# A two-layer hybrid trunk on one core: modulation sums by ones, rows ahead of weights, and rows on GpSimd's queue

## The chip, the core and the metric

The kernel runs on one core of a Trainium2 chip. A core has a matrix engine (TensorE, PE in the profile, whose weight loads are listed as PEld), a vector engine (VectorE, DVE), an activation engine (ScalarE, ACT), GpSimd (POOL) and a queue engine (SyncE, SP) that here does nothing but issue DMAs. Each engine takes its own instructions strictly in the order of its own list. Sixteen DMA engines move the data for all queues. The metric is the device time in microseconds, lower is better. It stands at 2661.34 us, the median of three runs (2660.47 to 2666.17).

## The reference, cut to what matters

```python
cond = jax.nn.silu(c)                                   # (1, 2048)
for l in range(2):
    mod = cond @ w_ada[l] + b_ada[l]                    # 6 vectors of 2048
    sh_m, sc_m, gt_m, sh_f, sc_f, gt_f = mod            # shift, scale, gate
    u = x * (1 + sc_m) + sh_m                           # x: (256, 2048)
    proj = u @ w_in[l]                                  # 4896 columns
    mix = concat(window_attention(proj), rwkv7(proj)) @ w_out[l]
    x = layer_norm(alpha * x + gt_m * mix)
    u = x * (1 + sc_f) + sh_f
    gate, up = split(u @ w_gate_up[l])                  # 2 x 5632 columns
    x = layer_norm(alpha * x + gt_f * ((silu(gate) * up) @ w_down[l]))
```

All weights are float32 and each is used once. `w_ada` alone is 2 x 2048 x 12288 numbers, 201 MB of the 622 MB that are read.

## The kernel before, in words

**Products.** Each float32 weight tile is split into a rounded part `hi` (ACT, line 430) and a remainder `lo` (DVE, line 431), and the activations are held as two such parts too. A product is three matmuls: high by high, high by `lo`, and the activation's remainder by high. `steps` (from line 415) loads a `raw` tile of 128 x 1024 (four buffers), makes `hi` (three buffers) and `lo` (two buffers), yields them to the matmuls, and then calls `pump`. `stream` (line 439) uses the weights as the moving operand, 512 columns at a time: lines 452, 453 (the one that reads `lo`) and 455. A step of two 512-column pieces and two token tiles is 12 matmuls. `tstream` (lines 464 to 466) uses the weights as the stationary operand.

**Modulation rows.** The six vectors per layer are not computed by matmul but on DVE: a tile `ast` holds 128 rows of `w_ada`, and `aacc += ast * cond[j]` runs once per row tile (line 265, in the opening line 353). 16 row tiles make one half of one vector, a unit. The sum over the 128 partitions follows in `ada_sums` (line 311): PE transposes each 128-column block (line 322), ACT sums each transposed block along its free side (line 326, one activation and one read of its accumulator), and DVE adds the bias (line 329) into `mods`. `pump` draws row tiles from one long generator at a set pace, so that the rows lie beside the weight streams: 0.75 of a draw per step in the feed-forward. The generator draws 20 times for a unit, of which 16 issue a row tile. `aacc` has one buffer in the feed-forward. An `ast` tile has two; its DMA stands on SP's queue (line 261), between the weights' DMAs (line 422).

**The opening.** The first two vectors of layer 0 (shift and scale) are needed before any matmul of `w_in`. `parts` (line 1355) makes them in five parts of 512, 512, 512, 256 and 256 columns. `ada_first` (line 340) loads the rows of both vectors of a part (line 348, eight buffers), DVE adds them up, `ada_sums` closes each vector, `make_u` transposes x and makes the activations `u` (lines 404 to 411), and `front` (line 513) runs the matmuls of that part over the 1696 columns that it holds.

**Order.** The program is built by a scheduler that orders instructions on every engine by its own simulated timeline, unless a dependence holds one back. So SP's queue is one list, in which rows, weights and small loads are mixed.

**Later.** In the mixer of layer 0 two units run by matmul instead (`ada_direct`, line 285: `cond` spread over 32 columns as stationary operand, the row tile as moving one, four at a time in four column groups of the array). `channel` holds the output projection and the feed-forward. Layer norm's reciprocal root is a power on GpSimd (line 1130), which does nothing else in the feed-forward.

Of the kernel before, what the change touches and what calls it, by code (L numbers as in the profile page):

```python
# [10 lines left out]
F32 = mybir.dt.float32  # L11
# [8 lines left out]
P = 128  # L20
D = 2048
# [23 lines left out]
PARTS = (4, 4, 4, 2, 2)  # L45
LAG = 2
WB = (4, 3, 2)
RED = 1
AR = (3, 7)
AA = (1, 45)  # L50
AP = (0.65, 0.3)
# [11 lines left out]
SPLIT_D = (1, 1)  # L63
WOFF, WPAD = 16, 64
TWO_PI = 2.0 * math.pi
IDLE = {"ada": 0, "first": 0, "dec": (0, 0), "ffn": (11, 6), "mix": 8}


@with_exitstack
def hybrid_trunk_kernel(  # L70
# [98 lines left out]
    def drv(l, nm, i, n=1):  # L169
        return der[l][:, DO[nm] + i:DO[nm] + i + n]  # L170

    def setup(sp, l, half, behind=None):

        prow = sp.tile([P, P], F32, tag="prow", bufs=2, name=f"prow{l}{half}")
# [76 lines left out]
    def ada_steps(l, mod, c0):  # L251

        src = w_ada[l].rearrange("(j p) n -> p j n", p=P)
        n0 = mod * D + c0
        if direct[0]:
            yield from ada_direct(l, mod, c0, src[:, :, n0:n0 + 1024])
            return
        acc = adap.tile([P, 1024], F32, tag="aacc", name="aacc")
        for j in range(KT):
            t = adap.tile([P, 1024], F32, tag="ast", name="ast", bufs=2)  # L260
            dma(t, src[:, j, n0:n0 + 1024])
            if j == 0:
                V.tensor_scalar_mul(acc, t, cond[:, 0:1])
            else:
                ins = V.scalar_tensor_tensor(acc, t, cond[:, j:j + 1], acc, ALU.mult, ALU.add)  # L265
# [6 lines left out]
        ada_sums(l, mod, c0, [acc[:, i * P:(i + 1) * P] for i in range(8)])  # L272
        done.add((l, mod, c0 // 1024))
        yield

    def ada_direct(l, mod, c0, src):
# [21 lines left out]
        row = adap.tile([P, T], F32, tag="aacc", name="grow")  # L298
        S.copy(row, gv[:, 0:T])
        turn[:] = 1, 1  # L300
        b = bank()
        for i in range(2):
            PE.transpose(b[:, i * P:(i + 1) * P], row[:, i * P:(i + 1) * P], ident)
        col = mod * KT + c0 // P
        bv = b[:, 0:T].rearrange("p (i q r) -> p q i r", q=4, r=32)
        V.scalar_tensor_tensor(mods[l][:, col:col + 8].rearrange("p (q i) -> p q i", q=4), bv[:, :, :, 0], 1.0 if mod in (1, 4) else 0.0,
                               prm(l, "b_ada", col, 8).rearrange("p (q i) -> p q i", q=4), ALU.add, ALU.add)
        done.add((l, mod, c0 // 1024))
        yield

    def ada_sums(l, mod, c0, blocks, idle=0):

        col = mod * KT + c0 // P
        n = len(blocks)
        sm = adap.tile([P, 8], F32, tag="asum", name="asum", bufs=2)
        for q in range(0, n, 4):
            b = bank()
            if q == 0:
                warm(b, idle)
            m = min(4, n - q)  # L320
            for i in range(m):
                PE.transpose(b[:, i * P:(i + 1) * P], blocks[q + i], ident)  # L322
            for i in range(m):
                bi = b[:, i * P:(i + 1) * P]
                if RED:
                    S.activation(bi, bi, AF.Copy, accum_out=sm[:, q + i:q + i + 1])
            if not RED:
                V.reduce_sum(sm[:, q:q + m], b[:, 0:m * P].rearrange("p (i k) -> p i k", k=P), axis=AX.X)
        V.scalar_tensor_tensor(mods[l][:, col:col + n], sm[:, 0:n], 1.0 if mod in (1, 4) else 0.0,
                               prm(l, "b_ada", col, n), ALU.add, ALU.add)  # L330
        if mod in (2, 5):
            row = adap.tile([8, P], F32, tag="arow", name="arow", bufs=2)[0:n]
            rb = bank()
            PE.transpose(rb[0:n, 0:P], mods[l][:, col:col + n], ident)
            S.copy(row, rb[0:n, 0:P])
            dma(gates[l, mod // 3, c0 // P:c0 // P + n], row)

    lead = []

    def ada_first(pool, c0, w):  # L340

# [3 lines left out]
        for j0 in range(0, KT, jj):  # L345
# [6 lines left out]
                else:  # L352
                    V.scalar_tensor_tensor(acc, t[:, j], cond[:, j0 + j:j0 + j + 1], acc, ALU.mult, ALU.add)
            yield
        for m in range(2):
            ada_sums(0, m, c0, [acc[:, m, i * P:(i + 1) * P] for i in range(w // P)], IDLE["ada"] if m == 0 and c0 + w == D else 0)

    done = set()

# [13 lines left out]
                       + halves(1, 5))  # L373
    pace = [0.0, 0.0]
    anchor = []
    direct = [False]

    def pump():

# [34 lines left out]
    def steps(srcs, W, kts, room=None, off=0):  # L414
# [3 lines left out]
        for i0 in range(0, len(kts), no):  # L418
            m = min(no, len(kts) - i0)
            raw = wp.tile([P, 1024], F32, tag="raw", name="raw", bufs=WB[0])  # L420
            for dst, src in srcs(raw[:, 0:m * W].rearrange("p (k w) -> p k w", w=W), kts[i0], m):
                dma(dst, src)
            if room:
                parts = [(raw[:, o * W:(o + 1) * W], *room()) for o in range(m)]
            else:
# [11 lines left out]
                    yield i0 + o, hi[:, o * W:(o + 1) * W], lo[:, o * W:(o + 1) * W]  # L437
            pump()

    def stream(srcs, W, kts, lhs, pieces, banks, first=True, last=True, ts=(0, 1), room=None, held=None):  # L440


        kept = []
        for i, hi, lo in held or steps(srcs, W, kts, room):
            kept.append((i, hi, lo))
            lt = lhs[i]
            st, sp_ = first and i == 0, last and i == len(kts) - 1
            for t in ts:
                xh, xl = lt[:, 0, t * P:(t + 1) * P], lt[:, 1, t * P:(t + 1) * P]
                for q, (c0, w) in enumerate(pieces):  # L450
                    bt = banks[t][q][:, 0:w]
                    PE.matmul(bt, lhsT=xh, rhs=hi[:, c0:c0 + w], start=st, stop=False)  # L452
                    PE.matmul(bt, lhsT=xh, rhs=lo[:, c0:c0 + w], start=False, stop=False)  # L453
                for q, (c0, w) in enumerate(pieces):
                    PE.matmul(banks[t][q][:, 0:w], lhsT=xl, rhs=hi[:, c0:c0 + w], start=False, stop=sp_)  # L455
        return kept

    def tstream(srcs, W, kts, us, blocks, first=True, last=True):
# [81 lines left out]
    def mixer(l, us, mixp, feeds):  # L540
# [99 lines left out]
        def decays(g):  # L640

            gsl = slice(g * T, (g + 1) * T)
            w2a2 = pa.tile([P, T], F32, tag="w2a2", name="w2a2", bufs=1)
            dma(w2a2[0:64, :], rwkv_w2[l, :, gsl])
            dma(w2a2[64:128, :], rwkv_a2[l, :, gsl])
# [534 lines left out]
    def channel(l, ys, wa, fp):  # L1180
# [77 lines left out]
                dma(out[0, t * P:(t + 1) * P, o:o + 512], zq)  # L1258

        gtf = fp.tile([P, D], F32, tag="gt", name="gtf")  # L1260
        wg = w_gate_up[l].rearrange("(k p) (s n) -> p k s n", p=P, s=2)
        first = True
        for lo_g, hi_g in ((0, 6), (6, 11)):
# [42 lines left out]
            for c0, w in ((0, 1024), (1024, 512), (1536, 512)):  # L1306
# [11 lines left out]
                for ts in ((0,), (1,)) if apart else ((0, 1),):  # L1318
# [5 lines left out]
                    for t in ts:  # L1324
# [8 lines left out]
                        if c0 == 1536 and not first:  # L1333
                            finish(t) if l + 1 == L else normalise(fp, z, t, stt[t])
            first = False
        if l + 1 == L:
            return None, None
        us = []
# [12 lines left out]
    with tc.tile_pool(name="pro", bufs=1) as pp:  # L1351
        xv = x[0].rearrange("(t p) d -> p t d", p=P)

        def parts():
# [23 lines left out]
            zt = pp.tile([P, 520], F32, name="zt")  # L1378
            G.memset(zt, 0.0)
            for t in tinv:  # L1380
                dma(t.rearrange("e s t -> (e s t)").rearrange("(p n) -> p n", p=P), zt)
# [38 lines left out]
```

## Time and profile before

| | us |
|---|---|
| median of three runs | 2661.34 |
| the profiled execution, its own time | 2673.23 |
| span of the profiled execution, first to last instruction | 2671.2 |
| PE busy | 2514.0 (94%) |
| VectorE busy | 1804.7 (68%) |
| ScalarE busy | 1186.5 (44%) |
| GpSimd busy | 146.7 (5%) |

The profiled execution is 11.9 us longer than the median and 2.0 us longer than its span. Read it by stages: the opening, up to the decays of the first mixer, where rows arrive; mixer 0, to 560; its output projection, to 640; the feed-forward of layer 0, 640 to 1400; mixer 1 and its projection; the feed-forward of layer 1, from 1960. Modulation rows run in the first four and in mixer 1 up to some 1700; in the last feed-forward there are none.

### The profile page before, as it was taken

What the parts mean: (1) busy time and instruction counts of PE and PEld (TensorE: products, weight loads), DVE (VectorE), ACT (ScalarE), POOL (GpSimd) and SP (SyncE); (2) the same over time, 40 slices, a digit from 0 to 9 for tenths busy, and PEclk for the clock granted to TensorE, in tenths of its full rate; (3) what the DMA queues carried; (4) which work ended last, traced back from release to release, by engine and by line L of the source; (5) the groups of instructions that cost most, each with busy time, mean ns of one, the idle gap of its engine ahead of it and who ended that gap; (6) DMA issues with size and microseconds to landing.
All of it is one profiled execution on the core that took longest, in us unless ns stands there. A gap on an engine that the chain in (4) does not pass through costs nothing.

```text
span 2671.2 us, 42267 instructions
## 1 busy us (share of the span) xinstructions
PE 2514.0 (94%) x15619; PEld 2090.1 (78%) x15619; DVE 1804.7 (68%) x2439; ACT 1186.5 (44%) x2023; POOL 146.7 (5%) x368
## 2 busy tenths in 40 slices
PE   3799998999999999999999998989899999999997
PEld 3697785677878888888788977867788888888887
DVE  7977766579877777677787776564855455545456
ACT  2464454435544444444454644543444443344442
POOL 1002212000000000000000024110000000000000
PEclk9899998999999999999999999988999999999999
DMA  9978658698998889888878785414655655566654
GB/s 371 358 215 253 202 176 266 207 335 301 327 328 303 309 301 317 284 299 304 293 247 291 218 264 148 129 50 179 221 189 184 195 184 196 195 190 188 191 189 149
DMA packets 336384, 637.51 MB, mean 239 GB/s; under 512 B 59510, under 2 KB 126514, under 8 KB 334642
## 3 DMA queue, kind: packets, MB, share of 16 engines
q1 hardware_dynamic: 333170, 629.05, 71.0%
q0 software_dynamic: 1280, 2.62, 0.4%
q10 hardware_dynamic: 1728, 3.15, 0.3%
q8 instruction: 122, 2.00, 0.3%
q14 instruction: 84, 0.69, 0.1%
HBM read 622.08 MB, written 12.62 MB: 238 GB/s over the span
## 4 chain that ended last, share of the span: by engine, by line
PE 62%; DMA 6%; DVE 5%; ACT 1%; issue 1%; POOL 0%; SPq 0%; DVEq 0%; ACTq 0%; POOLq 0%
PE acc L453 18%; PE acc L455 17%; PE acc L452 17%; DMA ast<-in_w_ada_dram 3%; DVE lo L431 2%; PE acc L465 1%; PE acc L466 1%; PE acc L464 1%; DMA raw<-in_w_gate_up_dram 1%; DVE aacc L265 1%; PE mb L1290 1%; DMA raw<-in_w_out_dram 1%; DMA raw<-in_w_in_dram 1%; PE mb L322 0%; DMA tm<-tinv 0%
## 5 line engine op out<-in xcount | busy, mean ns | idle before, releaser
L430 ACT CAST hi<-raw 128x1024 fp32r<-128x1024 f32 (+2 forms) x728 | 758.2, 1044 | 1093.2 <-PE acc L455 826.5
L431 DVE TENSOR_TENSOR lo<-raw,hi 128x1024 fp32r<-128x1024 f32 (+2 forms) x728 | 880.4, 1212 | 519.0 <-PE acc L453 350.1
L453 PE MATMUL acc<-lo,u 128*128 128x512 f32 x1568 | 515.7, 396 | 14.3 <-DVE lo L431 14.3
L455 PE MATMUL acc<-hi,u 128*128 128x512 f32 x1568 | 508.1, 392 | 0.0
L452 PE MATMUL acc<-hi,u 128*128 128x512 f32 x1568 | 460.1, 395 | 0.7 <-ACT u L410 0.7
L265 DVE SCALAR_TENSOR_TENSOR aacc<-ast,cond,aacc 128x1024 f32<-128x1024 f32 x270 | 345.7, 1280 | 105.8 <-DMA ast<-in_w_ada_dram 104.5
L453 PEld LDWEIGHTS acc<-lo,u 128*128 128x128 f32 x1568 | 294.2, 189 | 80.2 <-DVE lo L431 20.1
L452 PEld LDWEIGHTS acc<-hi,u 128*128 128x128 f32 x1568 | 296.3, 189 | 63.3 <-issue 1.2
L455 PEld LDWEIGHTS acc<-hi,u 128*128 128x128 f32 x1568 | 296.3, 189 | 61.9 <-issue 0.3
L453 PE MATMUL acc<-lo,ht 128*128 128x512 f32 (+1 forms) x720 | 243.7, 377 | 3.4 <-DVE lo L431 3.0
L455 PE MATMUL acc<-hi,ht 128*128 128x512 f32 (+1 forms) x720 | 242.2, 375 | 0.0
L452 PE MATMUL acc<-hi,ht 128*128 128x512 f32 (+1 forms) x720 | 217.1, 376 | 0.0
L464 PE MATMUL acc<-u,hi 128*128 128x256 f32 x720 | 201.1, 287 | 1.8 <-ACT hi L430 1.8
L465 PE MATMUL acc<-u,hi 128*128 128x256 f32 x720 | 201.3, 287 | 0.0
L466 PE MATMUL acc<-u,lo 128*128 128x256 f32 x720 | 188.7, 289 | 1.9 <-DVE lo L431 1.7
L453 PEld LDWEIGHTS acc<-lo,ht 128*128 128x128 f32 x720 | 135.1, 188 | 30.2 <-DVE lo L431 6.4
L455 PEld LDWEIGHTS acc<-hi,ht 128*128 128x128 f32 x720 | 135.6, 188 | 24.2
L452 PEld LDWEIGHTS acc<-hi,ht 128*128 128x128 f32 x720 | 134.8, 188 | 24.4
L464 PEld LDWEIGHTS acc<-u,hi 128*128 128x128 f32 x720 | 139.8, 194 | 4.5 <-ACT hi L430 2.0
L465 PEld LDWEIGHTS acc<-u,hi 128*128 128x128 f32 x720 | 139.6, 194 | 2.9 <-issue 1.6
L466 PEld LDWEIGHTS acc<-u,lo 128*128 128x128 f32 x720 | 130.7, 194 | 6.5 <-DVE lo L431 3.3
L1130 POOL TENSOR_TENSOR brs<-brs,mhalf 128x1 f32<-128x1 f32 x8 | 7.3, 916 | 1711.9 <-DVE brs L1129 776.6
(358 smaller groups left out, 2923.6 us busy)
## 6 DMA issues: line engine op xcount, KB each, us to landing
ast<-in_w_ada_dram SPq DMA_DIRECT2D x368, 512.0 KB
raw<-in_w_gate_up_dram SPq DMA_DIRECT2D x704, 256.0 KB
raw<-in_w_down_dram SPq DMA_DIRECT2D x176, 512.0 KB
raw<-in_w_in_dram SPq DMA_DIRECT2D x82, 512.0 KB
raw<-in_w_out_dram SPq DMA_DIRECT2D x64, 512.0 KB
raw<-in_w_in_dram SPq DMA_DIRECT2D x120, 256.0 KB
ast<-in_w_ada_dram SPq DMA_DIRECT2D x32, 256.0 KB
lnw<-in_ln_w_dram SPq DMA_DIRECT2D x4, 1024.0 KB
```

The source lines that it names most:

```text
L265: ins = V.scalar_tensor_tensor(acc, t, cond[:, j:j + 1], acc, ALU.mult, ALU.add)
L430: S.copy(h, fl)
L431: ins = V.tensor_tensor(r, fl, h.bitcast(F32), ALU.subtract)
L452: PE.matmul(bt, lhsT=xh, rhs=hi[:, c0:c0 + w], start=st, stop=False)
L453: PE.matmul(bt, lhsT=xh, rhs=lo[:, c0:c0 + w], start=False, stop=False)
L455: PE.matmul(banks[t][q][:, 0:w], lhsT=xl, rhs=hi[:, c0:c0 + w], start=False, stop=sp_)
L464: PE.matmul(bt, lhsT=hi[:, c0:c0 + w], rhs=xh, start=st and opens, stop=False)
L465: PE.matmul(bt, lhsT=hi[:, c0:c0 + w], rhs=xl, start=False, stop=False)
L466: PE.matmul(bt, lhsT=lo[:, c0:c0 + w], rhs=xh, start=False, stop=sp_ and closes)
L1130: G.tensor_tensor(rs[:, 0:1], rs[:, 0:1], mhalf[:, 0:1], ALU.pow)
L1290: PE.transpose(b[:, i * T + t * P:i * T + (t + 1) * P], hh[t][:, (2 * k2 + i) * P:(2 * k2 + i + 1) * P], ident)
```

## The change

1. `ada_sums` now works on column tiles: four matmuls with a column of ones, spread over 32 columns, as stationary operand put the sums of a quarter of the columns each into 32 partitions; one ACT copy, then two transposes (one for the 256-column parts), and the bias is added from PSUM. In the opening both vectors of a part are closed by one such group instead of two.
2. In the opening the DMAs of weights, of the decays' small weights, of the zeroing of a scratch, and of the first rows of the next vector are held behind the last modulation row issued so far.
3. In the feed-forward the row tiles' DMAs are issued from GpSimd's queue.
4. In the feed-forward of layer 0, `stream` issues all matmuls that read `lo` last in a step, for both token tiles.

```diff
+    def fetch(dst, src, later=True):
+        ins = dma(dst, src)
+        if later:
+            tc.add_manual_dep(ins.ins, lead[0], order, reason="behind the first modulation rows")
...
-            dma(t, src[:, j, n0:n0 + 1024])
+            if quiet[0]:
+                G.dma_start(t, src[:, j, n0:n0 + 1024])
+            else:
+                fetch(t, src[:, j, n0:n0 + 1024], j < 2 and not done)
...
+    def ada_sums(l, c0, acc, mods_, n):
+
+        gv, w = bank(), len(mods_) * n * P // 4
+        flat = acc if len(mods_) == 1 else None
+        for q in range(4):
+            blk = flat[:, q * w:(q + 1) * w] if flat is not None else acc[:, q // 2, q % 2 * w:(q % 2 + 1) * w]
+            PE.matmul(gv[32 * q:32 * q + 32, 0:w], lhsT=ones.to_broadcast([P, 32]), rhs=blk, start=True, stop=True)
+        row = (flat if flat is not None else acc[:, 0, :])[:, 0:w]
+        S.copy(row, gv[:, 0:w])
+        place(l, c0, row, mods_, w)
+
+    def place(l, c0, row, mods_, w):
+
+        b, m = bank(), w // P
+        for i in range(m):
+            PE.transpose(b[:, i * P:(i + 1) * P], row[:, i * P:(i + 1) * P], ident)
...
-        for q in range(0, n, 4):
-            b = bank()
...
-            for i in range(m):
-                PE.transpose(b[:, i * P:(i + 1) * P], blocks[q + i], ident)
-            for i in range(m):
-                bi = b[:, i * P:(i + 1) * P]
-                if RED:
-                    S.activation(bi, bi, AF.Copy, accum_out=sm[:, q + i:q + i + 1])
...
             for dst, src in srcs(raw[:, 0:m * W].rearrange("p (k w) -> p k w", w=W), kts[i0], m):
-                dma(dst, src)
+                ins = dma(dst, src)
+                if opening[0]:
+                    tc.add_manual_dep(ins.ins, lead[0], order, reason="behind the modulation rows of the part")
...
+            whole = late[0] and len(pieces) == 2
+            for part in [ts] if whole and 0 < i < len(kts) - 1 else [(t,) for t in ts]:
+                for t in part:
+                    xh, xl = lt[:, 0, t * P:(t + 1) * P], lt[:, 1, t * P:(t + 1) * P]
+                    for q, (c0, w) in enumerate(pieces):
+                        bt = banks[t][q][:, 0:w]
+                        PE.matmul(bt, lhsT=xh, rhs=hi[:, c0:c0 + w], start=st, stop=False)
+                        if not whole:
+                            PE.matmul(bt, lhsT=xh, rhs=lo[:, c0:c0 + w], start=False, stop=False)
+                    for q, (c0, w) in enumerate(pieces):
+                        PE.matmul(banks[t][q][:, 0:w], lhsT=xl, rhs=hi[:, c0:c0 + w], start=False, stop=sp_ and not whole)
+                for t in part if whole else ():
+                    for q, (c0, w) in enumerate(pieces):
+                        PE.matmul(banks[t][q][:, 0:w], lhsT=lt[:, 0, t * P:(t + 1) * P], rhs=lo[:, c0:c0 + w],
+                                  start=False, stop=sp_)
...
+        late[0] = l == 0
+        quiet[0] = True
...
+        quiet[0] = False
+        late[0] = False
...
+        opening[0] = True
         feeds = front(0, us, parts(), ahead=True)
+        opening[0] = False
```

What it does to the order is seen at three places. The first is SP's queue in the opening; `ast` are modulation rows, `raw` weights, `xt` a piece of x. Before, from the second piece of rows on:

```order
L348 DMA ast<-in_w_ada_dram 128x2x512 x2
L422 DMA raw<-in_w_in_dram 128x2x256
L348 DMA ast<-in_w_ada_dram 128x2x512
L422 DMA raw<-in_w_in_dram 128x2x128
L422 DMA raw<-in_w_in_dram 128x2x256
L348 DMA ast<-in_w_ada_dram 128x2x512
L422 DMA raw<-in_w_in_dram 128x2x128
L422 DMA raw<-in_w_in_dram 128x3x288
L348 DMA ast<-in_w_ada_dram 128x2x512
L422 DMA raw<-in_w_in_dram 128x288
```

The same place of the changed kernel:

```order
L357 DMA ast<-in_w_ada_dram 128x2x512 x2
L1388 DMA xt<-in_x_dram 128x2x512
L357 DMA ast<-in_w_ada_dram 128x2x512
L228 DMA posi<-in_positions_dram 128x2x1
L357 DMA ast<-in_w_ada_dram 128x2x512 x5
L430 DMA raw<-in_w_in_dram 128x2x256
L430 DMA raw<-in_w_in_dram 128x2x128
```

All 16 rows of the first part now stand ahead of the first weights.

The second place is PE in the feed-forward of layer 0, a step of 12 matmuls (before: lines 452 and 453 are high by high and high by `lo`, 455 the activation's remainder):

```order
L452 MATMUL acc<-hi,u 128x512 x4
L453 MATMUL acc<-lo,u 128x512 x2
L455 MATMUL acc<-hi,u 128x512 x2
L453 MATMUL acc<-lo,u 128x512 x2
L455 MATMUL acc<-hi,u 128x512 x2
```

The scheduler had already put the four high-by-high matmuls first, so a step read `lo` from its fifth matmul on. In the changed kernel lines 466, 470 and 473 are high by high, the remainder by high, and high by `lo`:

```order
L466 MATMUL acc<-hi,u 128x512 x2
L470 MATMUL acc<-hi,u 128x512 x2
L466 MATMUL acc<-hi,u 128x512 x2
L470 MATMUL acc<-hi,u 128x512 x2
L473 MATMUL acc<-lo,u 128x512 x4
```

The four matmuls that read `lo` moved to the end of the step: `lo` is first read by the ninth matmul and last by the twelfth (before, by the fifth and the tenth), and `hi` is last read by the eighth (before, by the twelfth).

The third place is GpSimd's list around the feed-forward of layer 0: the powers of the two layer norms (`brs`) stood next to each other before, and now frame the rows' DMAs:

```order
L1149 TENSOR_TENSOR brs<-brs,mhalf 128x1 x2
L266 DMA ast<-in_w_ada_dram 128x1024 x171
L1149 TENSOR_TENSOR brs<-brs,mhalf 128x1 x2
```

171 of the 288 row tiles of the later vectors left SP's queue.

More of the change, by code (lines that the diff above doesn't have):

```diff
@@ L47 @@
 WB = (4, 3, 2)
-RED = 1
 AR = (3, 7)
@@ L65 @@
 TWO_PI = 2.0 * math.pi
-IDLE = {"ada": 0, "first": 0, "dec": (0, 0), "ffn": (11, 6), "mix": 8}
+IDLE = {"first": 0, "dec": (0, 0), "ffn": (11, 6), "mix": 8}
 @with_exitstack
@@ L270, in ada_steps @@
             yield
-        ada_sums(l, mod, c0, [acc[:, i * P:(i + 1) * P] for i in range(8)])
+        ada_sums(l, c0, acc, (mod,), 8)
+        if mod in (2, 5):
+            gate_row(l, mod, c0, 8)
         done.add((l, mod, c0 // 1024))
@@ L300, in ada_direct @@
         turn[:] = 1, 1
-        b = bank()
[L302 to L307, printed above, removed]
+        place(l, c0, row, (mod,), T)
@@ L308, in ada_direct @@
         done.add((l, mod, c0 // 1024))
         yield
-    def ada_sums(l, mod, c0, blocks, idle=0):
-        col = mod * KT + c0 // P
-        n = len(blocks)
-        sm = adap.tile([P, 8], F32, tag="asum", name="asum", bufs=2)
-        for q in range(0, n, 4):
[L317 to L320, printed above, removed]
-            for i in range(m):
-                PE.transpose(b[:, i * P:(i + 1) * P], blocks[q + i], ident)
-            for i in range(m):
-                bi = b[:, i * P:(i + 1) * P]
-                if RED:
[L326 to L336, printed above, removed]
@@ L338, in hybrid_trunk_kernel @@
-    lead = []
+    def ada_sums(l, c0, acc, mods_, n):
[7 more added lines that the diff above has]
+        place(l, c0, row, mods_, w)
@@ new lines, in place @@
+    def place(l, c0, row, mods_, w):
+        b, m = bank(), w // P
+        for i in range(m):
+            PE.transpose(b[:, i * P:(i + 1) * P], row[:, i * P:(i + 1) * P], ident)
+        bv = b[:, 0:w].rearrange("p (i q r) -> p q i r", q=4, r=32)
+        nq = 4 // len(mods_)
+        for k, mod in enumerate(mods_):
+            col = mod * KT + c0 // P
+            V.scalar_tensor_tensor(mods[l][:, col:col + nq * m].rearrange("p (q i) -> p q i", q=nq), bv[:, k * nq:(k + 1) * nq, :, 0],
+                                   1.0 if mod in (1, 4) else 0.0,
+                                   prm(l, "b_ada", col, nq * m).rearrange("p (q i) -> p q i", q=nq), ALU.add, ALU.add)
@@ L340, in ada_first, with gate_row @@
+    def gate_row(l, mod, c0, n):
+        col = mod * KT + c0 // P
+        row = adap.tile([8, P], F32, tag="arow", name="arow", bufs=2)[0:n]
+        rb = bank()
+        PE.transpose(rb[0:n, 0:P], mods[l][:, col:col + n], ident)
+        S.copy(row, rb[0:n, 0:P])
+        dma(gates[l, mod // 3, c0 // P:c0 // P + n], row)
+    lead, opening = [], [False]
     def ada_first(pool, c0, w):
@@ L354, in ada_first @@
             yield
-        for m in range(2):
-            ada_sums(0, m, c0, [acc[:, m, i * P:(i + 1) * P] for i in range(w // P)], IDLE["ada"] if m == 0 and c0 + w == D else 0)
+        ada_sums(0, c0, acc, (0, 1), w // P)
     done = set()
@@ L375, in hybrid_trunk_kernel @@
     anchor = []
-    direct = [False]
+    direct, quiet = [False], [False]
     def pump():
@@ L438, in steps @@
             pump()
+    late = [False]
     def stream(srcs, W, kts, lhs, pieces, banks, first=True, last=True, ts=(0, 1), room=None, held=None):
@@ L447, in stream @@
             st, sp_ = first and i == 0, last and i == len(kts) - 1
[L448 to L455, printed above, removed]
+            whole = late[0] and len(pieces) == 2
[13 more added lines that the diff above has]
+                                  start=False, stop=sp_)
         return kept
@@ L643, in decays @@
             w2a2 = pa.tile([P, T], F32, tag="w2a2", name="w2a2", bufs=1)
-            dma(w2a2[0:64, :], rwkv_w2[l, :, gsl])
-            dma(w2a2[64:128, :], rwkv_a2[l, :, gsl])
+            fetch(w2a2[0:64, :], rwkv_w2[l, :, gsl], l + g == 0)
+            fetch(w2a2[64:128, :], rwkv_a2[l, :, gsl], l + g == 0)
             zb, ab = bank("zb"), bank("ab")
@@ L1380, in parts @@
             for t in tinv:
-                dma(t.rearrange("e s t -> (e s t)").rearrange("(p n) -> p n", p=P), zt)
+                fetch(t.rearrange("e s t -> (e s t)").rearrange("(p n) -> p n", p=P), zt)
+        opening[0] = True
         feeds = front(0, us, parts(), ahead=True)
+        opening[0] = False
     for l in range(L):
```

## The prediction

> **What bounds the kernel now.** I read the page's totals first, then the stages, then within each stage what waits.
>
> ```profile
> span 2671.2 us, 42267 instructions
> PE 2514.0 (94%) x15619; PEld 2090.1 (78%) x15619; DVE 1804.7 (68%) x2439; ACT 1186.5 (44%) x2023; POOL 146.7 (5%) x368
> ```
>
> PE is busy for 94% of the span, so only some 157 us are idle, and most of the time can move only where PE waits or gets less to do. The windows by stage show where that is (columns: stretch, its length, then busy time and instructions of PE, of its weight loads, of DVE, ACT and POOL, then the granted clock, the DMA share, GB/s):
>
> ```profile
> 0.00:35.69 35.69, 0.70 (x3) 0.36 (x3) 24.85 (x43) 4.17 (x5) 6.91 (x61) 1.00 0.98 350
> 35.69:43.54 7.85, 3.34 (x12) 2.14 (x13) 4.49 (x10) 4.33 (x21) 0.00 (x0) 1.00 1.04 397
> 43.54:134.05 90.51, 70.39 (x500) 65.63 (x501) 82.62 (x102) 37.78 (x87) 0.00 (x0) 0.89 1.04 367
> 134.05:160.00 25.95, 25.93 (x203) 25.64 (x204) 13.59 (x27) 12.42 (x25) 1.01 (x4) 0.91 0.60 171
> 160.00:560.00 400.00, 373.86 (x3538) 299.35 (x3537) 271.32 (x517) 188.00 (x432) 63.25 (x146) 0.94 0.73 233
> 640.00:1330.00 690.00, 683.39 (x3085) 561.27 (x3083) 522.34 (x497) 311.04 (x464) 0.00 (x0) 1.00 0.89 308
> 1400.00:1960.00 560.00, 518.85 (x4304) 433.95 (x4303) 382.33 (x695) 268.68 (x551) 70.16 (x151) 0.95 0.58 185
> 1960.00:2671.00 711.00, 697.47 (x3233) 582.48 (x3231) 369.87 (x369) 287.98 (x307) 2.15 (x2) 0.99 0.59 189
> ```
>
> The first four rows are the opening. Up to 134.05 the DMA engines are full and DVE is busy for 91% of the third row, while PE idles for 60 us. Then the picture turns: in the fourth row PE idles for 0.02 us of 25.95 and DMA falls to 0.60. So the opening has two laws in series: the rows of the five parts set 134.05, and behind it stands what PE has left to multiply. The feed-forward of layer 0 (640 to 1330) has only 6.6 us of idle PE; nothing there can gain more than that plus what PE is spared. The last feed-forward has no rows and keeps its order.
>
> **The opening.** PE's timeline, then DVE's, where each closing of a part's rows shows (start, length, instruction, and in brackets the idle time ahead of it and what ended that):
>
> ```profile
> 35.69 1.11 PE L322 MATMUL mb<-ident,aacc 128*128 128x128 f32 x4 [20.50 <-DVE aacc L353]
> 41.32 1.11 PE L404 MATMUL mb<-ident,xt 128*128 128x128 f32 x4 [1.72 <-ACT mb L326]
> 43.54 0.58 PE L464 MATMUL rk<-u,hi 128*128 128x256 f32 x1 [1.11 <-ACT u L410]
> ...
> 134.05 0.66 PE L322 MATMUL mb<-ident,aacc 128*128 128x128 f32 x2 [4.29 <-DVE aacc L353]
> ...
> 162.99 1.13 PE L649 MATMUL ab<-xwa,w2a 64*128 64x256 f32 x4
> ```
> ```profile
> 34.36 1.28 DVE L353 SCALAR_TENSOR_TENSOR aacc<-ast,cond,aacc 128x1024 f32<-128x1024 f32 x1
> ...
> 127.64 6.26 DVE L353 SCALAR_TENSOR_TENSOR aacc<-ast,cond,aacc 128x512 f32<-128x512 f32 x8
> 133.82 1.22 DVE L431 TENSOR_TENSOR lo<-raw,hi 128x1024 fp32r<-128x1024 f32 x1
> ```
>
> Counted from the shapes in SP's list, 11.49 MB were issued up to the last row of the first part and 9.51 MB now: 1.98 MB at the window's 350 GB/s are 5.7 us, so the first part's rows close at some 30 instead of 35.64. Then the sums. Before, from the first transposes to the first product 7.85 us passed. The new chain has four matmuls by ones, a copy, two transposes, and the 2.22 us from the x transposes to the first product, which stay (43.54 less 41.32). For the new operations the nearest rows are those of the mixer's row matmuls (32 columns, 256 wide; two records to a matmul, so 24 are three groups of four) and their copy:
>
> ```profile
> 487.24 1.50 PE L285 MATMUL gv<-ast,cond 128*32 128x256 f32 x24
> L299 ACT COPY grow<-gv x2: 372/372/373, 468.3 to 518.6; 128x256 f32<-128x256 f32 x2
> ```
>
> 0.50 for the four (1.50 / 3; on a cold array up to twice that), 0.37 for the copy, and 0.55 for two transposes (half of the 1.11 of L322 above): 3.6 to 4.2 with the 2.22. The first product comes at about 34 instead of 43.54. That alone ends nothing, since the rows of the later parts still rule. For the end of the fifth part there are two estimates. By bytes: up to its last row 47.33 MB were issued and now 46.15, and 1.18 MB at 367 GB/s are 3.2 us. By DVE: it starts 5.7 us sooner, but 24 remainders `lo` now stand ahead of that last row in its list instead of 22, and two at 1.22 take 2.4 back: 3.3. They agree on **-3.3**. Behind it, PE's list holds 164 products between the last sums and the decays (L648, L649; at 162.99), where it held 216. At 25.95 / 203 = 0.128 us each, 52 fewer are 6.6 us. Together 9.9; since the decays wait for a chain through ACT as well, I take **-9**, with bounds of -3 (the 52 come too late for their place, because their weights now stand behind rows) and -13 (the full 5.7 of the first part and the 6.6).
>
> **The remainders last.** In the first feed-forward the waits (us in total, times, longest) are:
>
> ```profile
> DVE aacc L265 <- DMA ast<-in_w_ada_dram: 63.2, 46, 4.0
> DVE lo L431 <- PE acc L453: 48.5, 36, 2.3
> PE acc L453 <- DVE lo L431: 6.2, 11, 1.1
> ```
>
> PE waits for `lo` for 6.2 us, nearly all of its 6.6 idle. `lo` was first read by the fifth matmul of a step and is now by the ninth. Four matmuls last 0.91 us:
>
> ```profile
> 665.32 0.87 PE mb L322 x8
> ...
> 682.71 0.91 PE acc L452 x4
> ```
>
> Against a longest wait of 1.1 us, 0.91 us of cover remove nearly all of each: **-5**. What is late next: `lo` is also released two matmuls later (by the twelfth, not the tenth), so DVE, which waits for that 48.5 us already, starts the next remainder up to 0.45 us later; but `hi` goes free four matmuls sooner. If this eats the cover, the term is 0; the whole idle time is -6.6.
>
> **The sums inside the feed-forward.** The 8 transposes of a unit cost PE 0.87 us. Now it is 0.50 and two transposes at 0.11: 0.72. Ten units lie in the stage (ten of L263, below), so **-1.5**, from 0 to -3. The 16 ACT instructions of a unit lie beside PE there (ACT is busy for 45% of the stage) and cost nothing, except where ACT ends the wait, once, in the output of the feed-forward (chain of waits):
>
> ```profile
> 1369.12 1.33 ACT wl L430 x4
> 1370.45 2.27 ACT mb L326 x16
> 1372.91 1.02 ACT wl L430 x3
> ```
>
> 2.27 us become one copy of 0.37; of the 1.9 I count **-1.5**, 0 to -2. There is a loss too. The feed-forward has one accumulator, and it is now held until the second transposes, which stand 23 or 24 matmuls behind the sums in PE's list (5.4 us at 0.227); the next unit's first operation waits for them on DVE, with remainders queued behind it:
>
> ```profile
> DVE aacc L263 <- PE mb L322: 4.3, 7, 1.0
> ```
>
> DVE's list answers by one or two remainders more ahead of that operation (a step of 12 matmuls, 2.7 us, each). What is left of the wait is 0 to 2.7 us per unit, up to 27 on DVE, whose slack in the stage is 168 (690 less 522): I count 0, and up to 5 in the range if half of the waits hit a remainder.
>
> **Rows on GpSimd's queue.** Issuing one costs SP 0.33 us, and SP waits there for free `ast` buffers with weights behind:
>
> ```profile
> L261 SPq DMA_DIRECT2D ast<-in_w_ada_dram x157: 327/328/750, 640.7 to 1328.0; - x157
> L793 POOL DMA_DIRECT2D tm<-tinv x16: 682/687/702, 237.6 to 1749.5; - x16
> DMA to landing us min/median/max: 2.8/3.6/6.9
> ```
>
> GpSimd takes 0.69 us for its nearest DMA (128 KB) and has nothing else to do in the stage: 157 x 0.69 = 108 of 690. Weights come freer, but PE waits for none of them here beyond the `lo` already counted. I take **0**; no gain beyond 6.6 exists, and the loss is the rival C. By the Trainium skill, DMA: Bandwidth & Descriptors, "Issuing engines are not separate DMA queues", issuing from several engines saves only the issuing time and the transfers interleave as before; by that this edit is worth nothing either.
>
> The mixers and the projection lose the same 16 ACT instructions per unit but are laid out anew by the scheduler; 0, with 4 us either way as an estimate (their idle PE is 26 and 41 us).
>
> **The sum.** -9 - 5 - 1.5 - 1.5 = -17. The profiled execution of 2673.2 would become 2656; it lies 11.9 above the median of the runs shown, and against that median of 2661.34 the forecast is **2644**.
>
> **The rivals.** *B, half of it.* The 52 products aren't ready early, since PE in the opening is also bound by weights, which are now behind rows; or the waits for `lo` turn into others, as by the accumulator that is held longer. For it: DVE, at 91%, makes rows and remainders alike. -3.3 in place of -9, or 0 for -5: about 2649 to 2650.
> *D, nothing.* Both of these, and 4 us lost in mixers laid out anew: 2661.3 - 3.3 - 3 + 4 = 2659. Against it: the 16 transposes and the ACT work are really gone.
> *C, slower: rows that land late.* There are two `ast` buffers, and 157 rows in 690 us leave 8.79 us for a buffer's round trip. DVE uses a row for 1.28 of them, so the stage becomes bound by rows from a mean landing of some 7.5 us (inside a unit, where 16 of 20 draws carry a row, from 5.75). The one GpSimd-issued DMA in this trace lands in 3.6, at most 6.9, with a quarter of the bytes; 384 KB more at 367 GB/s are 1.0, in a share of half the bandwidth 2.1: 4.6 to 5.7 at the median, so below. At a landing of 8 it would be 78.5 pairs x 9.28 = 728 instead of 690, and the median, with the opening's gain, 2661 + 38 - 10 = 2689. The point in its favour is that landing is already late: DVE waits 63.2 us for rows from SP.
> The Trainium skill has a rule for this, in SBUF — State Buffer, "SBUF: two separate sides": descriptors of a DMA issued from GpSimd can't be written while DVE runs an operation in a two-port mode, such as an fp32 copy or a tensor-scalar. Of DVE's work in the stage only this is of the kind:
>
> ```profile
> L263 DVE TENSOR_SCALAR aacc<-ast,cond 128x1024 f32<-128x1024 f32 x10 | 7.5, 752 | 4.3 <-PE mb L322 4.3
> ```
>
> 7.5 us of 690: where the rule holds, it delays a row by at most 0.75, ten times, and PE by nothing.
>
> **How the numbers follow.** The forecast, with its mechanisms at their sizes within some 6 us, has 0.47; B 0.22; D 0.16; C 0.15, half of it mild (some rows late, 2664 to 2675), half at 2689. A measurement can tell about 0.2% here, 5.3 us: faster is below 2656, slower above 2666.7. Faster: 0.47 + 0.22 and a little of D, 0.71; same: most of D and the edge of C, 0.16; slower 0.13. Range: down by the -13, the -6.6 and 4 of the mixers' scatter, partly together, to 2634; up to D and its scatter at 2664, which leaves out C.
>
> **What would show it.** First product near 34, last opening row near 130, decays near 153. In the first feed-forward: waits of PE for `lo` under 2 us, busy PE lower by 1.5, and DVE's wait for `ast` not above 63. ACT's stretch at 1370 shorter by 1.5. The forecast is wrong if GpSimd's rows land after 6 us or more, with PE then waiting for DVE behind them; if the fifth part closes at 134 as before; or if PE's waits reappear under `hi` or `raw`.

## The result, and the profile after

The changed kernel takes 2690.52 us (median of 4 runs, 2686.35 to 2692.92) against 2660.9 for the kernel before (4 runs): a ratio of 1.0106, interval 1.0082 to 1.0129. It is 30 us slower, where a time 17 us shorter was forecast, and it lies above the range of 2634 to 2664. The page of the changed kernel begins:

```profile
span 2691.2 us, 42092 instructions
...
PE 2523.0 (94%) x15671; PEld 2074.3 (77%) x15671; DVE 1802.4 (67%) x2439; ACT 1134.9 (42%) x1694; POOL 238.0 (9%) x539
```

ScalarE does 52 us less and GpSimd 91 more, as the change says; PE's share is the same. To see where the time went I use marks that both kernels have: the powers of the layer norms on GpSimd's timeline. They close the first mixer with its projection, and the first feed-forward. Before:

```profile
614.40 2.11 POOL L1130 TENSOR_TENSOR brs<-brs,mhalf 128x1 f32<-128x1 f32 x2 [94.41 <-issue]
1380.72 0.54 POOL L1130 TENSOR_TENSOR brs<-brs,mhalf 128x1 f32<-128x1 f32 x1 [764.21 <-DVE brs L1129]
```

And after:

```profile
616.75 0.55 POOL L1149 TENSOR_TENSOR brs<-brs,mhalf 128x1 f32<-128x1 f32 x1 [94.30 <-issue]
...
1407.52 0.56 POOL L1149 TENSOR_TENSOR brs<-brs,mhalf 128x1 f32<-128x1 f32 x1 [18.38 <-DVE brs L1148]
```

From mark to mark the first feed-forward lasted 766.3 us and now lasts 790.8. This stretch, **FFN** below, holds nearly all of the loss. The page of before needs one correction. Its profiled execution lay 12 us above the median, and most of the excess was in the second mixer: 533.2 us from the mark at 1380.72 to the next at 1913.88. In a second profiled execution of the same kernel the first layer norm came at 614.7, FFN lasted 764.6 and the second mixer 524.1; in the changed kernel it lasted 524.6. So 26 of the 30 us were lost in FFN, 2 ahead of it, and 2 in the last feed-forward.

The opening did nearly what was forecast. PE's timeline of the changed kernel:

```profile
30.66 1.08 PE L320 MATMUL mb<-aacc,ones 128*32 128x256 f32 x8 [15.99 <-DVE aacc L362]
35.88 0.58 PE L483 MATMUL rk<-u,hi 128*128 128x256 f32 x1 [1.11 <-ACT u L418]
...
130.53 0.42 PE L320 MATMUL mb<-aacc,ones 128*32 128x128 f32 x8
155.38 0.91 PE L667 MATMUL zb<-twd,w2a 64*128 64x256 f32 x3
```

The first product starts at 35.88 instead of 43.54 (forecast about 34), the sums of the fifth part at 130.53 instead of 134.05 (-3.5; forecast -3.3). The two products of the decays, L667 and L668, start at 155.38 and 156.04; before, the same two, L648 and L649, started at 164.50 and 162.99. Each is 7 to 9 us sooner, and the first of the pair, from which the forecast counted, 7.6. But the first layer norm is 2 us later than before, so all of that was lost again between the decays and that norm.

In the first feed-forward the waits of the changed kernel, from 640 to 1345 us, show who is late (us in all, times, longest):

```profile
ACT hi L440 <- DMA raw<-in_w_gate_up_dram: 131.6, 64, 7.5
DVE aacc L272 <- DMA ast<-in_w_ada_dram: 94.8, 70, 5.3
...
PEld acc L473 <- DVE lo L441: 25.9, 23, 2.3
PE acc L473 <- DVE lo L441: 17.0, 18, 2.0
```

VectorE waited 63.2 us for rows, now 94.8; PE waited 6.2 for `lo`, now 17.0. From mark to mark PE is busy for 760.0 of 790.8 us, before for 753.6 of 766.3: its idle time rose from 13 to 31 us. The 131.6 us that ScalarE waited for gate and up weights look like the largest change (37.4 before), but the runs below show that they come with the remainders last, which cost little.

### The profile page after: what moved, and what is told of

Its sections match the earlier page's. It is cut to its first block, busy times and chain, and to the rows that moved or that the text cites. A ratio compares the mean times of both kernels' runs of the same rounds, so it can differ in the third digit from the quotient of the medians.

```text
span 2691.2 us, 42092 instructions
## 1 busy us (share of the span) xinstructions
PE 2523.0 (94%) x15671; PEld 2074.3 (77%) x15671; DVE 1802.4 (67%) x2439; ACT 1134.9 (42%) x1694; POOL 238.0 (9%) x539
## 4 chain that ended last, share of the span: by engine, by line
PE 66%; DMA 18%; DVE 9%; issue 3%; POOL 2%; ACT 1%; SPq 1%; DVEq 0%; POOLq 0%; ACTq 0%
PE acc L466 16%; PE acc L470 16%; PE acc L468 12%; DMA ast<-in_w_ada_dram 11%; PE acc L473 5%; DVE lo L441 3%; PE acc L485 2%; PE acc L483 2%; PE acc L484 2%; DVE aacc L272 2%; DMA raw<-in_w_gate_up_dram 2%; DMA raw<-in_w_out_dram 1%; DMA tm<-tinv 1%; DMA raw<-in_w_down_dram 1%; DMA raw<-in_w_in_dram 1%
## 5 line engine op out<-in xcount | busy, mean ns | idle before, releaser
L470 PE MATMUL acc<-hi,u 128*128 128x512 f32 x1568 | 509.1, 392 | 0.0
L466 PE MATMUL acc<-hi,u 128*128 128x512 f32 x1568 | 483.3, 394 | 2.3 <-ACT hi L440 1.1
L468 PE MATMUL acc<-lo,u 128*128 128x512 f32 x864 | 289.1, 394 | 3.3 <-DVE lo L441 3.2
L470 PE MATMUL acc<-hi,ht 128*128 128x512 f32 (+1 forms) x720 | 243.6, 377 | 0.0
L466 PE MATMUL acc<-hi,ht 128*128 128x512 f32 (+1 forms) x720 | 225.4, 378 | 0.0
L473 PE MATMUL acc<-lo,u 128*128 128x512 f32 x704 | 196.2, 396 | 14.0 <-DVE lo L441 13.9
L468 PE MATMUL acc<-lo,ht 128*128 128x512 f32 (+1 forms) x544 | 189.4, 374 | 5.7 <-DVE lo L441 5.5
L483 PEld LDWEIGHTS acc<-u,hi 128*128 128x128 f32 x720 | 141.6, 197 | 14.2 <-ACT hi L440 10.9
L266 POOL DMA_DIRECT2D ast<-in_w_ada_dram x171 | 90.4, 529 | 679.2 <-DVE aacc L272 504.0
```

The lines of the kernel that those rows point to most:

```text
L266: G.dma_start(t, src[:, j, n0:n0 + 1024])
L473: PE.matmul(banks[t][q][:, 0:w], lhsT=lt[:, 0, t * P:(t + 1) * P], rhs=lo[:, c0:c0 + w], start=False, stop=sp_)
L483: PE.matmul(bt, lhsT=hi[:, c0:c0 + w], rhs=xh, start=st and opens, stop=False)
```

## The experiments

All were run beside the kernel before, whose median over 4 to 21 runs was between 2659.6 and 2664.8. "Decays" is the start on PE of the decay product that L648 issues before and L667 after, "norm" the first mark. The kernels whose code is that of before up to the feed-forward (before, the queue, the remainders, the third buffer) have norms between 609.2 and 616.1, so a few microseconds there tell nothing.

| kernel | median us | ratio, interval | decays | norm | FFN us |
|---|---|---|---|---|---|
| before, two executions | 2660.9 | 1 | 164.5, 163.9 | 614.4, 614.7 | 766.3, 764.6 |
| the change | 2690.52 | 1.0106 (1.0082 to 1.0129) | 155.4 | 616.8 | 790.8 |
| without GpSimd's queue | 2675.53 | 1.0064 (1.0044 to 1.0083) | 155.0 | 612.8 | 776.1 |
| without remainders last | 2694.89 | 1.0140 (1.0117 to 1.0163) | 152.4 | 614.0 | 791.7 |
| without later sums by ones | 2707.31 | 1.0180 (1.0156 to 1.0205) | 158.1 | 619.2 | 786.5 |
| before + GpSimd's queue | 2679.43 | 1.0073 (1.0046 to 1.0100) | 164.3 | 614.1 | 786.2 |
| before + remainders last | 2672.60 | 1.0044 (1.0027 to 1.0061) | 165.4 | 609.2 | 768.2 |
| sums by ones alone | 2682.12 | 1.0086 (1.0062 to 1.0111) | 163.4 | 621.1 | 778.3 |
| opening alone | 2674.87 | 1.0053 (1.0036 to 1.0070) | 156.5 | 620.9 | 762.3 |
| queue + third row buffer | 2666.14 | 1.0006 (0.9986 to 1.0025) | 163.7 | 616.1 | 761.9 |
| before + third row buffer | 2654.04 | 0.9953 (0.9935 to 0.9971) | 164.2 | 612.6 | 757.0 |
| the change + third row buffer | 2660.57 | 0.9989 (0.9974 to 1.0004) | 152.9 | 609.0 | 766.6 |
| sums by ones, own row tile | 2672.25 | 1.0040 (1.0027 to 1.0053) | 163.2 | 617.5 | 769.5 |
| opening, sums by ones, third buffer, row tile | 2656.41 | 0.9987 (0.9972 to 1.0002) | 152.7 | 607.7 | 761.6 |

### Each part undone, and the queue alone

The queue undone, then the remainders, then the later sums:

```diff
-        quiet[0] = True
```


> The changed kernel with one part undone: the feed-forward's modulation rows are issued from SP's queue again. Watched is the first feed-forward, from the first layer norm's power on GpSimd to the next layer norm's: 766.3 us before (614.40 to 1380.72), 790.8 in the changed kernel (616.75 to 1407.52). Theory Q (rows on GpSimd's queue and weights on SP's now compete and both land late): 766 to 772 us, a total near 2668, and ScalarE's wait for gate and up weights back from 132 us to some 40. Theory L (remainders last let DVE start each remainder later) and theory H (the accumulator held through copy and transposes): it stays at 788 to 792 and the total near 2690.


```diff
-        late[0] = l == 0
```


> The changed kernel with the matmuls of a step in the old order of the code again (remainders not last). Theory L: first feed-forward 766 to 772 us, total near 2668, PE's waits for lo back from 17 to some 6 us. Theories Q and H: 788 to 795 us, total 2688 to 2695 (up to 5 us above the changed kernel, if the cover of 0.91 us that I counted on exists).


```diff
-        ada_sums(l, c0, acc, (mod,), 8)
+        ada_sums_old(l, mod, c0, [acc[:, i * P:(i + 1) * P] for i in range(8)])
```


> The changed kernel with the old sums (eight transposes, eight activations and accumulator reads) for all units behind the opening; the opening's joint sums by ones stay. Theory H: first feed-forward 766 to 775 us, total near 2670. Theories Q and L: 789 to 794 us, total 2690 to 2694, since PE gets the 0.15 us per unit back and the 16 ScalarE instructions return.

And the kernel before with the queue alone:

```diff
-            dma(t, src[:, j, n0:n0 + 1024])
+            (G.dma_start if quiet[0] else dma)(t, src[:, j, n0:n0 + 1024])
```


> The kernel before with one part of the change alone: the feed-forward's modulation rows are issued from GpSimd's queue. Theory Q: first feed-forward 785 to 795 us instead of 766, total 2680 to 2690, rows landing at a median of 5.4 us and ScalarE waiting over 100 us for weights. Theories L and H: 764 to 768 us, total within 4 us of 2661.

The queue alone makes FFN 20 to 22 us longer (786.2), and undone it gives 14.7 back (776.1). With the remainders in the old order FFN stays within 1 us of the changed kernel's (791.7), so theory L falls. The sums undone give back 4.3 us, far less than theory H had said. That kernel is nevertheless the slowest, 17 us above the changed kernel, and this was not foreseen: its second mixer lasts 542.4 us instead of 524.6, and why stays open. The queue is the first cause, but the 776.1 that stay without it are 10 above before: a second one is left.

One sign of theory Q is missing. With the queue alone ScalarE waits 47.4 us for gate and up weights (its line is shown under "A third row buffer"), not over 100; with the queue undone it still waits 105.2, and with the remainders last alone 111.8.

### The rest, one part at a time

The kernel before, unchanged, profiled once more:

> The kernel before, unchanged, profiled once more. Its first profiled execution lies 12 us above its median, the other kernels' within 3 us of theirs, and its second mixer with the projection lasts 533.2 us from layer norm to layer norm where the changed kernel and three variants show 522 to 525 (542 with the old sums). If that execution was an odd one there, this one shows 520 to 526, a first feed-forward of 764 to 768, and a span near 2660. If it shows 533 again, the change does gain some 9 us in the second mixer.

The first execution was the odd one: this one has 524.1 us for the second mixer, and a span of 2660.9.

Remainders last alone (the new `stream` with `late[0] = l == 0`, put into the kernel before):

> The kernel before with one part of the change alone: in the first feed-forward the matmuls that read the remainders come last in a step. Theory L (this causes the 10 us by which the first feed-forward stays longer, 776.1, when the rows are back on SP's queue): first feed-forward 772 to 778, total near 2668. Theory S (the sums by ones cause them, by holding the accumulator) or cover of 0.91 us as I forecast: 760 to 767, total 2655 to 2661.

Sums by ones alone (the changed kernel without `quiet`, `late`, `opening` and the dependence in `fetch`):

> The changed kernel with the sums by ones alone: rows on SP's queue, remainders in the old order, the opening's loads not held behind rows. Theory S: first feed-forward 772 to 778 us. Theory L: 763 to 768. In both the decays of the first mixer start between 157 and 164 us (164.50 before, 155.38 in the changed kernel, 152.39 without the remainders last), as the joint sums alone shorten the chain but not the rows' way.

The opening alone (the changed kernel without `quiet` and `late`, with the old sums for later units):

> The opening's part of the change alone: joint sums by ones and rows ahead of weights there; behind it the old sums, rows on SP's queue, the old order of remainders. Decays at 153 to 158 us. If the opening's gain reaches the end, the first layer norm comes at 604 to 607 and the total at 2651 to 2654. If the first mixer takes it back by itself (by its waits for rows or small loads), the layer norm stays at 611 to 617 and the total at 2656 to 2664. First feed-forward 764 to 768 in both.

The sums cost FFN 12 to 14 us (778.3), as theory S said; the opening costs it nothing (762.3). Remainders last cost 2 to 4 (768.2, between the two theories), near the case in which the forecast put the term at 0 and far from its -5. The whole program is 0.44% slower with them; its profiled execution has 8 us more in the second mixer, whose time varies by as much in one and the same program (below), so what the other runs of it lost is not settled. The opening alone is 15 us slower than before although it starts the decays 7.4 us sooner. In its profiled execution the first layer norm comes 6 us later; that execution is the fastest of its six, 6 us under their median, so where the others lost the rest isn't seen.

### A third row buffer

In the feed-forward every third row tile gets a buffer of its own, once with rows on GpSimd's queue, once on SP's:

```diff
-            t = adap.tile([P, 1024], F32, tag="ast", name="ast", bufs=2)
+            t = third[0].tile([P, 1024], F32, tag="ast3", name="ast", bufs=1) if quiet[0] and j % 3 == 2 else adap.tile([P, 1024], F32, tag="ast", name="ast", bufs=2)
```


> The kernel before with the feed-forward's rows on GpSimd's queue, as in the run of the queue alone (first feed-forward 786.2 us, total 2679), and a third buffer for the row tile in the feed-forward. Theory R (the round trip of a row buffer, issue plus a landing of 5.4 us plus its use on VectorE, has become the pace of the stage): first feed-forward back to 762 to 770 us, total 2655 to 2665, and VectorE's wait for rows down from 93 to under 40 us. Theory X (rows and weights share the DMA engines worse from two queues) or theory O (the scheduler's list for this queue places rows and remainders worse): 782 to 792 us, total 2675 to 2685.

> The kernel before with the third row buffer alone, rows on SP's queue. Theory R, applied to SP's rows too (VectorE waits 65 to 69 us for them): first feed-forward 758 to 763 us instead of 765, total 2652 to 2660, no more than PE's 12 us of idle time there allow. Under theories X and O: 763 to 768, total within 3 us of 2660.

With the queue alone, the waits in FFN were:

```profile
POOL ast L261 <- DVE aacc L265: 528.9, 149, 13.5
...
DVE aacc L265 <- DMA ast<-in_w_ada_dram: 92.7, 55, 4.5
ACT hi L430 <- DMA raw<-in_w_gate_up_dram: 47.4, 22, 7.0
```

With the third buffer as well:

```profile
POOL ast L261 <- DVE aacc L265: 499.7, 148, 13.6
...
DVE aacc L265 <- DMA ast<-in_w_ada_dram: 2.5, 3, 1.0
```

FFN falls from 786.2 to 761.9, while the rows land no sooner (median 5.4 without, 5.6 with the third buffer):

```profile
DMA to landing us min/median/max: 3.7/5.6/7.9
```

So theory Q had the right part of the change but not the mechanism: most of the cost came from two buffers against a round trip, not from two queues that share the DMA engines. SP's rows were at that limit already. In the second execution of before VectorE waited for them as follows, from mark to mark:

```profile
DVE aacc L265 <- DMA ast<-in_w_ada_dram: 69.2, 49, 3.5
```

With the third buffer on SP's queue:

```profile
DVE aacc L265 <- DMA ast<-in_w_ada_dram: 1.7, 4, 0.9
```

FFN falls to 757.0, and the kernel is 0.47% faster than before. This run is also the fair control of the one with queue and third buffer: beside it the queue still costs 4.9 us in FFN (761.9) and 12 in the total (2666.14 against 2654.04). So with three buffers the queue costs 5 us where it cost 20 with two; the round trip accounts for some 15, and theories X and O can stand only for what is left, which no run divides.

What the other queue adds to a round trip is seen at two rows. The kernel before (its second execution): VectorE frees a row buffer, SP issues the next row, and VectorE takes the row of the issue at 705.07 at 710.48:

```profile
703.76 1.28 DVE L265 SCALAR_TENSOR_TENSOR aacc<-ast,cond,aacc 128x1024 f32<-128x1024 f32 x1
...
710.48 1.28 DVE L265 SCALAR_TENSOR_TENSOR aacc<-ast,cond,aacc 128x1024 f32<-128x1024 f32 x1 [1.20 <-DMA ast<-in_w_ada_dram]
```
```profile
705.07 0.33 SPq L261 DMA_DIRECT2D ast<-in_w_ada_dram  x1
```

The same with the queue alone changed; the row issued at 700.81 is taken at 707.31:

```profile
699.24 1.28 DVE L265 SCALAR_TENSOR_TENSOR aacc<-ast,cond,aacc 128x1024 f32<-128x1024 f32 x1
...
707.31 1.28 DVE L265 SCALAR_TENSOR_TENSOR aacc<-ast,cond,aacc 128x1024 f32<-128x1024 f32 x1 [1.36 <-DMA ast<-in_w_ada_dram]
```
```profile
700.81 0.53 POOL L261 DMA_DIRECT2D ast<-in_w_ada_dram  x1 [3.18 <-DVE aacc L265]
```

SP issues 0.03 us after the buffer is free (703.76 + 1.28 = 705.04), GpSimd 0.29 after (700.52), and it issues for 0.53 instead of 0.33 us. From free to taken it is 5.44 and 6.79 us. These two rows lie further apart than most: counted in the same way over all rows that VectorE waited for from 640 us to the end of the rows, the medians are 5.7 us (46 rows) and 6.3 (51 rows), so the queue adds some 0.6 us.

### The held accumulator

The whole change with the third buffer, and the sums by ones alone with a tile of their own for the copied sums in the feed-forward:

> The whole change with a third row buffer in the feed-forward. Theory R and H (the feed-forward loses by the rows' round trip, and the held accumulator only shortens the time into which that must fit): first feed-forward from 790.8 to 755 to 766 us, total 2655 to 2667. If the sums cost PE or VectorE time by themselves: 770 to 776 us, total near 2672. If queue contention were the cause: 785 or more.


```diff
-        row = (flat if flat is not None else acc[:, 0, :])[:, 0:w]
+        row = free[0].tile([P, T], F32, tag="frow", name="frow", bufs=1) if free[0] else (flat if flat is not None else acc[:, 0, :])[:, 0:w]
```


> The sums by ones alone, as before (first feed-forward 778.3 us, total 2682), but in the feed-forward ScalarE copies the sums to a tile of their own, so that the accumulator is free after the four matmuls by ones and no longer held through copy and transposes. Theory H (the hold makes the next unit's rows late): first feed-forward 763 to 769 us, total 2668 to 2673. Theory P (the sums cost PE time or are laid out worse): 775 to 780 us, total 2678 to 2683.

The own tile takes FFN from 778.3 to 769.5, 8.8 of the 12 to 14 us, and VectorE's waits for rows fall from 83.5 to 70.5: theory H, with 3 to 5 us left that may be PE's or the layout's. In the changed kernel the hold is seen on PE's timeline; sums and transposes of one unit are 5.9 us apart, and the accumulator is free only behind the second:

```profile
882.89 0.64 PE L320 MATMUL mb<-aacc,ones 128*32 128x256 f32 x8
888.81 0.38 PE L329 MATMUL mb<-ident,aacc 128*128 128x128 f32 x2
```

With the third buffer the whole change has an FFN of 766.6 instead of 790.8, at the level of before, and the total falls by 30 us to 2660.57. So one more row buffer removes a loss as large as the whole. It is not all explained by that: beside the kernel before with the same third buffer (757.0), the change still costs 9.6 us in FFN, which no run divides among sums, queue and remainders. Round trip and hold work on the same limit, since the hold shortens the time into which 16 round trips must fit. That would be why the sums cost 13 us alone but only 4.3 on top of the queue; no run shows it by itself.

### Where the opening's gain goes

The chain of the changed kernel between the decays and the first use of the inverse matrices (`m`):

```profile
192.82 1.21 DVE aacc L272
194.05 5.15 DMA ast<-in_w_ada_dram
...
204.44 5.34 DMA ast<-in_w_ada_dram
209.88 1.36 DVE aacc L272
211.25 5.04 DMA ast<-in_w_ada_dram
...
231.16 6.23 DMA qkv<-stg
```

It runs through rows again. To test that, work is left out, in the kernel before and in the opening alone: of the first unit behind the opening only two row tiles are loaded, and VectorE's operations use these.

```diff
+            if not done and j >= 2:
+                t = kept2[j % 2]
...
```


> The kernel before with work left out: of the first unit of rows behind the opening only the first two row tiles are loaded; VectorE's 16 operations stay, on these two tiles. This is the control of the next run. Decays near 164, the first layer norm between 606 and 614 us (614.4 and 614.7 with all loads).

> The opening's part of the change alone, with the same work left out: of the first unit behind the opening only two row tiles are loaded. Theory W (between 190 and 229 us VectorE takes those rows at the pace at which they land, whenever the decays came, and so the opening's 8 us wait there): with the loads gone the first use of the inverse matrices, at 241.4 us with them and 242.2 before, comes 5 to 8 us ahead of the control's, and the layer norm 4 to 8 us ahead of it. Theory M (the first mixer takes it back elsewhere, by ScalarE's and VectorE's chains or the granted clock): the gap at that point is under 3 us, or it is there and gone again by the layer norm.

At `m` the opening's lead was 0.9 us with the loads (241.35 against 242.22) and is 5.1 without them (234.74 against 239.84): theory W holds so far. But by the first layer norm the lead has become a lag of 13 us (619.1 against 606.1), as theory M has it, and the medians are 2687.11 us with the opening and 2667.42 for the control (ratios to before 1.0103 and 1.0023). Most of the lag is there by the projection's first matmul (511.2 against 496.2), though this point isn't quite the same in both: from the first row matmul to it PE has 790 instructions with the opening and 720 without, because the control's scheduler left some row matmuls for later. The granted clock in that stretch was 0.87 with the opening and 0.99 without. How much is the clock and how much the other order stays open.

### What can be kept

The changed kernel with rows back on SP, remainders in the old order, third row buffer and own row tile:

> The changed kernel with rows on SP's queue, remainders in the old order, a third row buffer and a separate row tile for the sums in the feed-forward; the opening and the sums by ones stay. If theories R and H are whole and the opening's gain is kept by the first mixer: first feed-forward 755 to 760 us, layer norm at 604 to 608, total 2644 to 2650. If the mixer takes the gain back, as in the runs so far: feed-forward the same, layer norm at 610 to 616, total 2652 to 2658, no better than the third buffer alone (2654.04).

The decays come at 152.7 and the layer norm at 607.7, 5 us ahead of the kernel with the third buffer alone; its feed-forward is 4.6 us longer (761.6 against 757.0), and the median of 2656.41 is not better than 2654.04, nor is the ratio to the kernel before (0.9987 against 0.9953). So here some of the opening's gain may have reached the layer norm in the profiled execution, though 5 us is no more than norms scatter here, and none is seen in the total.

## Why the prediction was wrong

- **Rows on GpSimd's queue: the failed step.** It was costed at 0, because PE waited for no weights beyond `lo` and because the landing was estimated at 4.6 to 5.7 us, below a threshold of 5.75 inside a unit. The landing was inside that estimate, 5.4 at the median and up to 8.8. But the 5.75 us are all the time from a free buffer to a row that is taken, and the prediction filled them with the landing alone: it left out the issue (0.53 us) and the start behind the freeing instruction (0.29). Measured from free to taken, rows that VectorE waited for took 6.3 us on GpSimd's queue, above 5.75, and 5.7 on SP's, already at it. VectorE's 63.2 us of waits for rows had shown that limit. The cost was 20 us, some 15 of which the third buffer removes. Rival C had the mechanism and was given 0.15. Its 2689, so near to the measured 2690.52, is luck: it stands for a landing of 8 us and for an opening's gain of 10 that reaches the end, and the changed kernel loses 16 us even with the queue undone.
- **The held accumulator: counted at 0, up to 5.** It cost 9 of the sums' 13 us when they were alone. VectorE's slack of 168 us was held against it, but slack on average did not help: VectorE waited for rows, 83.5 us with the hold and 70.5 without, since a row buffer comes free only after its row has gone into the accumulator.
- **Remainders last: -5 forecast, between -1 and +4 measured.** With them alone PE's waits for `lo` did not fall (6.7 and 2.6 us on the two lines, against 7.5 to 8.2 before, from mark to mark). The prediction named a later start of VectorE as the case in which the term is 0. That this ate the cover is not shown: VectorE's wait for a free `lo` rose from 48.5 to 54.5 us, but its waits for rows rose too, from 65.3 to 83.0.
- **The opening: nearly right at the decays** (-7.6 from first product to first product; -9 forecast), wrong at the end. The chain from the first sums to the first product took 5.2 us instead of 3.6 to 4.2. The forecast carried the gain through to the total without asking what bounds the first mixer. In the test, with the loads of the next unit of rows left out, 5.1 us of lead stood at `m` where 0.9 stood with them; what took the rest behind `m` is not settled.
- **PE's and ScalarE's savings by the sums** (-1.5 each) can't be told apart from the hold in these runs.
- **The mixers:** 4 us either way was too little. In the second mixer alone, two executions of the kernel before differ by 9.

The rule of the Trainium skill on queues (DMA: Bandwidth & Descriptors, "Issuing engines are not separate DMA queues") was weighed as "no gain". The run agrees with no gain, but the issue time of which the rule speaks got longer here, 0.53 instead of 0.33 us, and counted because it stood in a round trip.

## What to carry to other kernels

Where an engine off the bound waits often and shortly for a double-buffered transfer, the stage may be at the limit of that round trip, as it was here. Count free, issue, land and use against the pace before moving the transfer to another queue, and try a third buffer first. A temporary that is written back into the buffer it came from holds that buffer until its last reader is done, with everything that stands ahead of that reader. A gain at the start of a program is a gain only if the next stage waits for the part that came earlier.

## What the runs showed of the hardware

In the first feed-forward a row tile of 512 KB takes 0.53 us to issue from GpSimd, and the issue starts some 0.3 us behind the instruction that frees its buffer; on SP it was 0.33 and 0.03 (medians over some 155 rows each, with the queue alone and in the second execution of before). The granted clock in the mixers differs between executions of one and the same program. In two executions of the kernel before, the windows of the second mixer from 350 us behind its first mark (the third figure from the end is the clock):

```profile
1730.70:1780.70 50.00, 41.00 (x432) 31.85 (x430) 31.73 (x102) 20.63 (x65) 14.31 (x38) 0.80 0.27 75
1780.70:1830.70 50.00, 45.30 (x408) 33.61 (x409) 28.82 (x97) 24.07 (x73) 1.64 (x1) 0.90 0.09 27
```
```profile
1729.30:1779.30 50.00, 41.16 (x435) 31.81 (x435) 31.59 (x102) 20.65 (x66) 14.30 (x38) 0.86 0.27 77
1779.30:1829.30 50.00, 45.30 (x416) 34.97 (x415) 31.49 (x100) 26.59 (x77) 1.64 (x1) 1.00 0.18 56
```

The first, at 0.80 and 0.90, is 9 us longer in this mixer than the second, at 0.86 and 1.00. The clock goes with the time, but that it makes all of the 9 us is not shown. In the feed-forward, at a clock of 1.00, the same two executions agree within 2 us, so marks there tell small changes apart better than marks behind a mixer.
